# Picking the gathered tile's experts for four heads at once, with index lookups two slots innermost and a new pacing of the gate stage

## The chip, the cores and the metric

The kernel runs on one core of a Trainium2 chip. The metric is the device time of one execution in microseconds; the time given is the median of several runs. In all texts PE is TensorE, DVE is VectorE, ACT is ScalarE, POOL is GpSimd, SP is SyncE, the engine that issues most DMAs.

## What is computed

Two decoder layers over 512 tokens of width 1024 and 16 meta tokens ahead of them. A layer is a mixer (causal pooling in layer 0, stick-breaking attention in layer 1) and then a PEER expert network, which takes most of the time:

```python
def peer(h, w_query, sub_keys, u, v):          # 8 heads, 2 x 128 sub-keys, 16384 experts
    q = (h @ w_query).reshape(tokens, 8, 2, 128)
    s = einsum('thpc,hpnc->thpn', q, sub_keys)            # two rows of 128 scores a head
    top_s, top_i = lax.top_k(s, 16)
    cand_s = top_s[..., 0, :, None] + top_s[..., 1, None, :]          # 256 candidates
    cand_i = top_i[..., 0, :, None] * 128 + top_i[..., 1, None, :]
    best_s, best_pos = lax.top_k(cand_s, 16)
    expert = take_along_axis(cand_i, best_pos); gate = softmax(best_s)
    act = gelu(einsum('td,thkd->thk', h, u[expert]), approximate=False)
    return einsum('thk,thkd->td', gate * act, v[expert])
```

Each token so has 128 experts with a gate, 16 of each of 8 heads.

## The kernel before

**Two ways through the experts.** The 512 tokens are four tiles of 128. Tiles 0 to 2 are "dense": the products with all 16384 experts are formed on PE, and those not picked get a gate of zero. Tile 3 (`GATHERED`) and, in layer 0, the meta tokens fetch the rows of just the experts that were picked. A row, in the words of the program, is one slot of the gathered tile: 128 tokens' expert vectors u and v, 128x2048 f32, fetched by an indirect DMA that POOL issues (L343) into one of `NROW` = 4 buffers with at most three in flight; DVE forms the dot product `prod` with the tokens (L355), ACT its gelu `ga` (L359), DVE the weight `gwt` (L363) and the update `hx` of the residual (L367). The gathered tile has 128 rows a layer, the meta tokens 16. Four calls of `row_step` take one row through: fetch, dot, gelu, update.

**The query stage.** For each of 8 heads two projections (PE, `psu`, L510 and L511) are copied out by ACT (`qt`, L512, 3 buffers), and their product with the keys (`ps`, L524) is copied by ACT to `s` (L527, 3 buffers), of which DVE takes the top 16 of each of 8 rows of scores (`top16`, L393 to L397). After each head, tile 3's slots are picked (`select`, below), and some steps of rows are run. Between heads stand u steps (`u_step`, L314): 24 matmuls that form one block of 128 experts' products with the three dense tiles, of which the result goes to DRAM (`aout`). A weight of a projection or a u step is split into two parts, `w_hi` by ACT (L279) and `w_lo`, on POOL in the query stage (L283) and on DVE in the gate stage (L281), two buffers each. POOL's queue so holds the w_lo of the query stage and the gathers, in the order of the program.

**A pick.** `select` takes the sums of the two sorted lists that can be among the best 16 (80 of the 256, `cand`), their top 16 a head (values `bv`, positions `bp`), works out of the position the two ranks (`da`, `db`, some 14 small instructions), looks each rank up among the 16 indices of its list (a one-hot of 16 a slot, L442; its product with the indices, L445; a sum, L448), and forms the softmax gate. It is called once a head for tile 3 (16 slots), once for the meta tokens, and in the gate stage once for each dense tile (128 slots).

**The gate stage.** For each dense tile `build_gates` writes, 8 tokens at a time, two one-hots and a weighed one (`hot` L604, `weighed` L608 twice), from which PE forms the gates of all experts (`pg`, L588); they go through ACT (`stage`) to DRAM (`gout`). The stage is a generator that yields a planned cost after each piece: in a dense pick 3.0 twice, 3.5, 6.0 twice and 1.0 (22.5 in all), and 2.44 for each of the 16 groups of a tile (39 in all). The planner adds each cost times `DVE_SLACK` to `td`, and then issues quarters of u steps (`u_parts`, 24 matmuls in four parts) until their planned time `tu` reaches `td`; a u step is planned at `ucost` = 0.0111 x 384 = 4.26, and a gate group's PE work at 0.47 for four tokens. It runs row steps until `tr` reaches `td`; each adds `ROW_PERIOD[layer][0] / 8` to `tr` and 4.7 / 8 to `td`. Rows stop when fewer than `QUIET` = 8 groups are left. What DVE and PE do in this stage stands in each queue in the order that this sets.

**The v stage.** The u steps that are left (`late`) come each with two `v_step`s, the first three ahead; when no u step is left, v steps follow alone ("lone"). A v step loads 128 experts' v, their products and gates (`v32`, `ac2` and, for four blocks, `gt`, from SP's queue), splits them (`v_hi`, `v_lo`, `wt_hi`, `wt_lo`) and runs 18 matmuls (L705) into sums that stay in PSUM. Each step adds `ucost` to `tu`, and a row step `ROW_PERIOD[layer][1] / 8` to `tr`. After the last row the lone v steps go on without rows.

## Time and profile before

| what | value |
|---|---|
| median of 3 runs | 3092.58 us (3089.8 to 3094.88) |
| the profiled execution, device time | 3092.34 us |
| its span | 3090.6 us |
| mean granted clock of PE over the span | 0.979 |
| layer 0, query stage to the first gate product | 57 to 314 us |
| layer 0, gate stage | 314 to 656 us |
| layer 1, the same two | 1780 to 2038, 2038 to 2382 us |

The span runs from the first to the last instruction of the profiled execution, the device time a little beyond it on either side. Engines work side by side, so a busy share says which of them is near its limit over all, and not at which moment; for that the stretches are looked at one by one. The four stretches above are cut by the first gate product (`pg`) and the end of the gates' writing; what lies behind 656 us is layer 0's v stage and the attention, and behind 2382 us layer 1's v stage.

### The profile page before, as it was taken

How to read it: one execution, taken by the hardware profiler on the slowest of the kernel's cores; microseconds unless marked ns; L12 is line 12 of the kernel's file. 1: busy time of each engine (PE TensorE's matmuls, PEld its weight loads, DVE VectorE, ACT ScalarE, POOL GpSimd, SP SyncE). 2: the span in 40 equal slices, each digit the busy share in tenths (PEclk: the TensorE clock that was granted, in tenths of full speed). 3: DMA queues.
4: the chain of work that ended last, by engine and by line, in shares of the span. 5: the costliest groups of instructions: out<-in, count | busy, mean ns of one | idle time of the engine just before them, and what ended most of it. 6: DMA issues, size and time to landing. Idle time of an engine off the chain costs nothing.

```text
span 3090.6 us, 45463 instructions
## 1 busy us (share of the span) xinstructions
PE 2926.3 (95%) x16514; PEld 2609.5 (84%) x16514; DVE 2412.3 (78%) x5158; ACT 1344.7 (44%) x2190; POOL 694.7 (22%) x702
## 2 busy tenths in 40 slices
PE   8988899989999999999999989888999999999999
PEld 7887898988888888779965778788898888888887
DVE  3999999878878887856456469999987988888755
ACT  3443655643333333344455334454645433333333
POOL 3431221121212111004235244312211122121100
PEclk9999999999999999999999999999999999999999
DMA  3535789899999998942100344478878999999775
GB/s 128 181 122 205 288 286 336 295 347 351 338 324 335 334 348 291 316 148 82 56 1 1 109 156 146 166 279 277 319 291 315 391 326 337 324 341 342 256 226 170
DMA packets 290451, 763.61 MB, mean 247 GB/s; under 512 B 23601, under 2 KB 180529, under 8 KB 252081
## 3 DMA queue, kind: packets, MB, share of 16 engines
q1 hardware_dynamic: 224416, 393.48, 37.7%
q0 software_dynamic: 39168, 285.23, 25.0%
q10 hardware_dynamic: 26640, 82.00, 6.7%
q8 instruction: 129, 2.11, 0.3%
q14 instruction: 98, 0.79, 0.1%
HBM read 676.54 MB, written 84.08 MB: 246 GB/s over the span
## 4 chain that ended last, share of the span: by engine, by line
PE 71%; DVE 21%; issue 3%; DMA 2%; ACT 2%; POOL 0%; SPq 0%; DVEq 0%; ACTq 0%; POOLq 0%
PE y L705 32%; PE psu L314 24%; PE pp L124 2%; PE pp L125 2%; PE pp L123 2%; DVE w_lo L281 2%; PE pg L588 2%; DVE weighed L608 2%; DVE hot L604 2%; DVE prod L355 2%; DVE hx L367 1%; DVE mr L395 1%; DVE ti L397 1%; DVE ti L394 1%; DMA w<-in_peer_ut_dram 1%
## 5 line engine op out<-in xcount | busy, mean ns | idle before, releaser
L314 PE MATMUL psu<-n_hi,w_lo 128*128 128x384 f32 x2048 | 704.3, 344 | 66.5 <-DVE w_lo L281 66.5
L343 POOL DMA_INDIRECT row<-in_peer_uv_dram,ei x272 | 392.6, 1443 | 1641.8 <-DVE hx L367 1238.5
L314 PE MATMUL psu<-n_hi,w_hi 128*128 128x384 f32 x2048 | 713.2, 348 | 11.8 <-ACT ac L321 7.2
L314 PE MATMUL psu<-n_lo,w_hi 128*128 128x384 f32 x2048 | 704.8, 344 | 0.6 <-DVE n_lo L118 0.6
L279 ACT ACTIVATE w_hi<-w 128x1024 fp32r<-128x1024 f32 x288 | 304.9, 1060 | 471.1 <-PE psu L314 358.9
L705 PE MATMUL y<-v_hi,wt_hi 128*128 128x512 f32 x1536 | 474.9, 390 | 6.4 <-ACT wt_hi L697 5.8
L705 PE MATMUL y<-v_lo,wt_hi 128*128 128x512 f32 x1536 | 474.7, 390 | 2.2 <-DVE v_lo L691 2.0
L705 PE MATMUL y<-v_hi,wt_lo 128*128 128x512 f32 x1536 | 474.2, 390 | 0.0
L314 PEld LDWEIGHTS psu<-n_hi,w_lo 128*128 128x128 f32 x2048 | 395.2, 193 | 76.4 <-DVE w_lo L281 76.1
L314 PEld LDWEIGHTS psu<-n_hi,w_hi 128*128 128x128 f32 x2048 | 393.1, 192 | 17.7 <-ACT ac L321 8.0
L314 PEld LDWEIGHTS psu<-n_lo,w_hi 128*128 128x128 f32 x2048 | 394.0, 192 | 4.9 <-DVE n_lo L118 1.1
L697 ACT ACTIVATE wt_hi<-wt 128x384 fp32r<-128x384 f32 x256 | 134.4, 525 | 570.9 <-PE y L705 275.4
L698 DVE TENSOR_TENSOR wt_lo<-wt,wt_hi 128x384 fp32r<-128x384 f32 x256 | 142.5, 557 | 267.7 <-ACT wt_hi L697 267.5
L705 PEld LDWEIGHTS y<-v_lo,wt_hi 128*128 128x128 f32 x1536 | 288.5, 188 | 64.8 <-DVE v_lo L691 4.4
L705 PEld LDWEIGHTS y<-v_hi,wt_lo 128*128 128x128 f32 x1536 | 288.7, 188 | 60.9 <-DVE wt_lo L698 0.4
L705 PEld LDWEIGHTS y<-v_hi,wt_hi 128*128 128x128 f32 x1536 | 287.3, 188 | 60.5 <-ACT wt_hi L697 6.2
L367 DVE SCALAR_TENSOR_TENSOR hx<-row,gwt,hx 128x1024 f32<-128x1024 f32 x256 | 336.5, 1314 | 2.1
L355 DVE SCALAR_TENSOR_TENSOR prod<-row,hnat 128x1024 bf16<-128x1024 f32 x272 | 333.6, 1226 | 0.7 <-DMA row<-in_peer_uv_dram,ei 0.6
L281 DVE TENSOR_TENSOR w_lo<-w,w_hi 128x1024 fp32r<-128x1024 f32 x230 | 280.7, 1221 | 65.9 <-ACT w_hi L279 64.6
L691 DVE TENSOR_TENSOR v_lo<-v,v_hi 128x1024 fp32r<-128x1024 f32 x256 | 312.2, 1220 | 7.9 <-ACT v_hi L690 7.9
L690 ACT ACTIVATE v_hi<-v 128x1024 fp32r<-128x1024 f32 x256 | 270.5, 1056 | 23.5 <-DMA v<-in_peer_uv_dram 23.2
L593 ACT ACTIVATE stage<-pg 128x512 f32<-128x512 f32 x192 | 200.7, 1157 | 79.7 <-PE pg L588 77.3
(312 smaller groups left out, 4258.4 us busy)
## 6 DMA issues: line engine op xcount, KB each, us to landing
w<-in_peer_ut_dram SPq DMA_DIRECT2D x256, 512.0 KB
v<-in_peer_uv_dram SPq DMA_DIRECT2D x256, 512.0 KB
gout<-stage ACTq DMA_DIRECT2D x24, 2048.0 KB
gt<-gout SPq DMA_DIRECT2D x64, 768.0 KB
aout<-ac ACTq DMA_DIRECT2D x161, 192.0 KB
ac<-aout SPq DMA_DIRECT2D x161, 192.0 KB
w<-in_peer_wq_dram SPq DMA_DIRECT2D x32, 512.0 KB
wn<-in_w_kv_dram SPq DMA_DIRECT2D x8, 1024.0 KB
```

Of the source, the lines that this page charges most:

```text
L279: amark.append(sc.activation(whi, w, AF.Copy))
L281: vmark.append(v.tensor_sub(wlo, w, whi.bitcast(F32)))
L314: m = pin(pe.matmul(ps[:, :ND], a[:, k, :], b[:, k, c0:c0 + ND], start=st, stop=en))
L343: gp.indirect_dma_start(out=row, out_offset=None, in_=peer_uv, in_offset=bass.IndirectOffsetOnAxis(ap=item[1], axis=0))
L355: v.scalar_tensor_tensor(prod, row[:, :D], 1.0, hn_nat[i], ALU.mult, ALU.mult, accum_out=dot)
L367: v.scalar_tensor_tensor(acc, row[:, D:], wt, acc, ALU.mult, ALU.add)
L593: sc.activation(stage[:, :, o:o + 4].rearrange("p j t -> p t j"), pg, AF.Copy, scale=1.0 / GSCALE)
L690: amark.append(sc.activation(vhi, v32, AF.Copy))
L691: vmark.append(v.tensor_sub(vlo, v32, vhi.bitcast(F32)))
L697: sc.activation(whi, wt, AF.Copy)
L698: vmark.append(v.tensor_sub(wlo, wt, whi.bitcast(F32)))
L705: pe.matmul(y[n][half], wp[:, ts], vq[:, half * 512:(half + 1) * 512], start=st, stop=en)
```

## The change

**Picks.** Tile 3's slots are picked for four heads at once (`GH`), behind heads 3 and 7; the first row of tile 3 can so be fetched only when head 3 has its scores. The planner's allowance for rows is 26 for each of the heads from the fifth on, where it was 10.4 for every head.

**Lookups.** In all picks the ranks `da` and `db` become F16; the one-hot is laid out with two slots innermost, compared with `iota_x` (each number twice), and the indices `tib` are written twice as wide to fit; the product of 16 is halved by an addition before the reduction, whose input is half as long.

**Pacing.** The planned costs of a pick become 6.9, 5.6, 3.4, 4.6 twice and 1.2 (26.3 in all), `DVE_SLACK` 1.27; in the gate stage a row step adds 23 / 8 to `tr`, where it was 18 / 8, and 0.95 to `td`, where it was 4.7 / 8. The period of the v stage stays 13.5.

```diff
-DVE_SLACK = 1.35
+DVE_SLACK = 1.27
-ROW_PERIOD = ((18.0, 13.5), (18.0, 13.5))
+ROW_PERIOD = ((18.0, 23.0, 13.5), (18.0, 23.0, 13.5))
+GH = 4
...
             def gather_rows(i, h, i1, i2, gate, ns, acc, first):
-                ef = gr.tile([P, TK], F32, name="ef", bufs=2)
+                ef = gr.tile([P, GH * TK], F32, name="ef")[:, :ns]
                 v.tensor_scalar(ef, i1, float(NK), float(layer * NE), ALU.mult, ALU.add)
-                ei = gr.tile([P, TK], I32, name=f"ei{i}_{h}")
+                ei = gr.tile([P, ns], I32, name=f"ei{i}_{h}")
...
                         if h % 4 == 3:
-                            yield 3.0
-                    a, b, u, w = st("da"), st("db"), st("du"), st("dw")
+                            yield 6.9 if h == 3 else 5.6
+                    a, b, u, w = st("da", F16), st("db", F16), st("du"), st("dw")
...
-                    yield 3.5
-                    tib = tmp.tile([P, nh, 2, TK], F16, name=f"tib{nh}")
-                    v.tensor_copy(tib, tii)
+                    yield 3.4
+                    tib = tmp.tile([P, nh * 2, TK, 2], F16, name=f"tib{nh}")
+                    v.tensor_copy(tib, tii.rearrange("p h c a -> p (h c) a").unsqueeze(3).to_broadcast(
+                        [P, nh * 2, TK, 2]))
+                    t5 = tib.rearrange("p (h c) a b -> p h c (a b)", c=2)
...
-                        v.tensor_tensor(oh, iota_b.unsqueeze(1).to_broadcast([P, ns, TK]),
-                                        sel.unsqueeze(2).to_broadcast([P, ns, TK]), ALU.is_equal)
-                        o4 = oh.rearrange("p (h s) a -> p h s a", h=nh)
-                        v.tensor_tensor(o4, o4, tib[:, :, half, :].unsqueeze(2).to_broadcast([P, nh, TK, TK]),
-                                        ALU.mult)
+                        oh = flat.rearrange("p (n a b) -> p n a b", a=TK, b=2)
+                        v.tensor_tensor(oh, iota_x[:, :TK].unsqueeze(1).to_broadcast([P, ns // 2, TK, 2]),
+                                        sel.rearrange("p (n b) -> p n b", b=2).unsqueeze(2).to_broadcast(
+                                            [P, ns // 2, TK, 2]), ALU.is_equal)
+                        o4 = flat.rearrange("p (h n c) -> p h n c", h=nh, c=2 * TK)
+                        v.tensor_tensor(o4, o4, t5[:, :, half, :].unsqueeze(2).to_broadcast(
+                            [P, nh, TK // 2, 2 * TK]), ALU.mult)
+                        o3 = flat.rearrange("p (n c) -> p n c", c=2 * TK)
+                        v.tensor_add(o3[:, :, :TK], o3[:, :, :TK], o3[:, :, TK:])
                         ir = outp.tile([P, ns], F32, name=f"{tag}i{half}")
-                        v.tensor_reduce(ir, oh, AX.X, ALU.add)
+                        v.tensor_reduce(ir.rearrange("p (n b) -> p n b", b=2),
+                                        oh[:, :, :TK // 2, :].rearrange("p n a b -> p n b a"), AX.X, ALU.add)
                         res.append(ir)
-                        yield 6.0 * nh / H
+                        yield 4.6 * nh / H
...
-                    yield 1.0
+                    yield 1.2
...
-                        tq += 10.4
+                        tq += 26.0 if h >= GH else 0.0
...
-                        for i in gathered:
-                            res = []
-                            for _ in select(qp, gr, f"g{i}_{h}", tv[i][:, h:h + 1], ti[i][:, h:h + 1], 1, res):
-                                pass
-                            gather_rows(i, h, *res, TK, hx[i], False)
+                        if h % GH == GH - 1:
+                            hs = slice(h - GH + 1, h + 1)
+                            for i in gathered:
+                                res = []
+                                for _ in select(qp, gr, f"g{i}_{h}", tv[i][:, hs], ti[i][:, hs], GH, res):
+                                    pass
+                                gather_rows(i, h, *res, GH * TK, hx[i], False)
...
                     while tr < td and blocks[0] >= QUIET and row_step():
-                        tr += ROW_PERIOD[layer][0] / 8
-                        td += 4.7 / 8
+                        tr += ROW_PERIOD[layer][1] / 8
+                        td += 0.95
```

**What moves.** PE's instructions are the same in number (17,576 matmuls of the program); DVE's go from 4303 to 3952. By the order of the program the stages hold:

| | layer 0 before | now | layer 1 before | now |
|---|---|---|---|---|
| rows ahead of the first gate group / in the gate stage / in the v stage | 15 / 31 / 98 | 17 / 27 / 100 | 14 / 31 / 83 | 16 / 27 / 85 |
| u steps done ahead of the v stage, of 128 | 79 | 86 | 82 | 90 |
| w_lo on DVE ahead of the first group / in the gate stage / after | 13 / 59 / 46 | 15 / 64 / 39 | 10 / 59 / 43 | 12 / 65 / 35 |
| lone v steps with rows among them / rows there | 20 / 14 | 44 / 30 | 5 / 5 | 32 / 22 |
| v steps after the last row | 20 | 10 | 41 | 30 |

On POOL, in layer 0's query stage, the first rows of tile 3 (`ei_0`, head 0's slots) stand between the w_lo of early heads before:

```order
L283 TENSOR_TENSOR w_lo<-w_1183,w_hi 128x1024
L343 DMA row<-in_peer_uv_dram,ei_0_988 128x2048 x3
L283 TENSOR_TENSOR w_lo<-w_1217,w_hi 128x1024
L343 DMA row<-in_peer_uv_dram,ei_0_988 128x2048
L283 TENSOR_TENSOR w_lo<-w_1323,w_hi 128x1024
L343 DMA row<-in_peer_uv_dram,ei_0_988 128x2048
L283 TENSOR_TENSOR w_lo<-w_1383,w_hi 128x1024
```

Now the first rows (`ei_3`, the slots of heads 0 to 3) come behind the w_lo of head 5's first projection (`w_1872`), and that of its second (`w_1935`) behind five of them:

```order
L282 TENSOR_TENSOR w_lo<-w_1872,w_hi 128x1024
L342 DMA row<-in_peer_uv_dram,ei_3_1688 128x2048 x5
L282 TENSOR_TENSOR w_lo<-w_1935,w_hi 128x1024
L282 TENSOR_TENSOR w_lo<-w_1995,w_hi 128x1024
L342 DMA row<-in_peer_uv_dram,ei_3_1688 128x2048 x3
L282 TENSOR_TENSOR w_lo<-w_2147,w_hi 128x1024
```

Before, three gathers stood together at first and then one between two w_lo each; now five, then three, with buffers for four rows.

On DVE, in layer 0 before, one row is worked on inside each head's pick (here that of head 3: the lookup of `db`, then the row's update, then head 4's top 16):

```order
L355 SCALAR_TENSOR_TENSOR prod,dot<-row,hnat_88 128x1024
L442 TENSOR_TENSOR oh_1866<-iota_b,db 128x256
L445 TENSOR_TENSOR oh_1866<-oh_1866,tib_1859 128x256
L448 TENSOR_REDUCE g_3i_1869<-oh_1866 128x16
L334 TENSOR_TENSOR ei_3_1881<-ef,g_3i_1869 128x16
L363 TENSOR_TENSOR gwt<-ga,g_0gate 128x1
L367 SCALAR_TENSOR_TENSOR hx_76<-row,gwt,hx_76 128x1024
L393 MAX tv_633<-s 128x8 x2
```

Now the first rows come at the end of head 4's top 16, several in a row:

```order
L396 MAX_INDEX ti_638<-tv_634,mr_1860 128x8
L394 MATCH_REPLACE mr_1866<-tv_634,s 128x128
L354 SCALAR_TENSOR_TENSOR prod,dot<-row,hnat_87 128x1024
L395 MAX tv_634<-mr_1866 128x8
L354 SCALAR_TENSOR_TENSOR prod,dot<-row,hnat_87 128x1024
L396 MAX_INDEX ti_638<-tv_634,mr_1866 128x8
L362 TENSOR_TENSOR gwt<-ga,g_3gate 128x1 x2
L366 SCALAR_TENSOR_TENSOR hx_75<-row,gwt,hx_75 128x1024 x2
L354 SCALAR_TENSOR_TENSOR prod,dot<-row,hnat_87 128x1024
```

So the rows moved from the heads' picks to the end of a top 16 that is complete but for its last indices.

On DVE, late in layer 1's v stage, the lone v steps before have no row among them:

```order
L698 TENSOR_TENSOR wt_lo<-wt,wt_hi 128x384
L693 TENSOR_TENSOR wt<-ac_30021,gt 128x384
L691 TENSOR_TENSOR v_lo<-v_29957,v_hi 128x1024
L698 TENSOR_TENSOR wt_lo<-wt,wt_hi 128x384
L693 TENSOR_TENSOR wt<-ac_30053,gt 128x384
```

At the place that answers to it now the rows go on:

```order
L354 SCALAR_TENSOR_TENSOR prod,dot<-row,hnat_17483 128x1024
L699 TENSOR_TENSOR v_lo<-v_28702,v_hi 128x1024
L362 TENSOR_TENSOR gwt<-ga,g_7gate 128x1
L701 TENSOR_TENSOR wt<-ac_28779,gt 128x384
L366 SCALAR_TENSOR_TENSOR hx_75<-row,gwt,hx_75 128x1024
L706 TENSOR_TENSOR wt_lo<-wt,wt_hi 128x384
```

The u steps run out earlier, and the rows go on beside v steps alone.

## Rows read from the trace of the kernel before

**Rows 1.** The page's first part: busy time and instructions of each engine.

```profile
PE 2926.3 (95%) x16514; PEld 2609.5 (84%) x16514; DVE 2412.3 (78%) x5158; ACT 1344.7 (44%) x2190; POOL 694.7 (22%) x702
```

**Rows 2.** Stretches: length; busy PE, PEld, DVE, ACT, POOL; clock; DMA share; GB/s.

```profile
57.00:314.00 257.00, 222.41 (x1473) 217.44 (x1473) 230.04 (x1071) 102.65 (x180) 83.76 (x44) 0.93 0.48 166
314.00:656.00 342.00, 317.88 (x2252) 304.46 (x2250) 307.50 (x506) 196.25 (x263) 61.88 (x32) 0.98 0.84 304
1220.00:1283.00 63.00, 61.79 (x270) 50.21 (x269) 51.40 (x77) 22.92 (x38) 9.32 (x8) 1.00 0.93 322
1240.00:1280.00 40.00, 38.79 (x169) 31.16 (x168) 33.66 (x53) 15.67 (x26) 7.36 (x6) 1.00 0.98 341
...
2038.00:2382.00 344.00, 313.34 (x2212) 299.87 (x2211) 305.33 (x515) 195.72 (x261) 62.67 (x31) 0.97 0.83 296
2410.00:2450.00 40.00, 40.00 (x195) 35.30 (x194) 36.72 (x54) 15.81 (x26) 9.34 (x7) 1.00 1.04 398
```

**Rows 3.** PE's waits, 57 to 314: line, releaser: total us, times, longest.

```profile
PE ps L524 <- ACT qt L512: 15.7, 7, 5.1
PE psu L314 <- DVE w_lo L281: 14.0, 5, 7.8
PE psq L511 <- ACT w_hi L279: 4.3, 1, 4.3
```

**Rows 4.** PE's waits, 314 to 656.

```profile
PE psu L314 <- DVE w_lo L281: 17.6, 10, 3.1
```

**Rows 5.** DVE's waits, 314 to 656.

```profile
DVE w_lo L281 <- ACT w_hi L279: 24.3, 10, 7.0
```

**Rows 6.** DVE in time, head 2 of layer 0: start, us, line.

```profile
125.44 0.49 DVE L393 MAX8 tv<-s 128x8 f32<-128x128 f32 x2 [1.11 <-issue]
...
134.34 0.25 DVE L408 TENSOR_TENSOR cand<-tv 128x16 f32<-128x16 f32 x2
...
135.33 0.24 DVE L393 MAX8 bv<-cand 128x8 f32<-128x80 f32 x1
...
136.67 1.42 DVE L453 TENSOR_TENSOR dd<-bv 128x16 f32<-128x16 f32 x1
...
143.40 0.18 DVE L334 TENSOR_TENSOR ei<-ef,g_2i 128x16 int32<-128x16 f32 x1
...
143.68 3.28 DVE L367 SCALAR_TENSOR_TENSOR hx<-row,gwt,hx 128x1024 f32<-128x1024 f32 x1
```

**Rows 7.** DVE by shape, 57 to 403: count, busy us, mean ns.

```profile
L281 DVE TENSOR_TENSOR w_lo<-w,w_hi 128x1024 fp32r<-128x1024 f32 x26 | 31.6, 1220 | 2.8 <-ACT w_hi L279 2.6
L355 DVE SCALAR_TENSOR_TENSOR prod<-row,hnat 128x1024 bf16<-128x1024 f32 x23 | 28.0, 1218 | 0.6 <-DMA row<-in_peer_uv_dram,ei 0.6
L608 DVE TENSOR_TENSOR weighed<-hot,sl 128x1024 f16<-128x1024 f16 x32 | 20.6, 685 | 0.0
L604 DVE TENSOR_TENSOR hot<-iota_x,sl 128x2048 f16<-128x2048 f16 x16 | 19.4, 1220 | 0.0
L448 DVE TENSOR_REDUCE gdi<-hot 128x128 f32<-128x2048 f16 x3 | 6.8, 2279 | 0.0
...
L442 DVE TENSOR_TENSOR hot<-iota_b,da 128x2048 f16<-128x2048 f16 x2 | 4.6, 2284 | 0.0
```

**Rows 8.** In time: head 3's scores, an update, head 7's last index.

```profile
143.76 2.39 PE L524 MATMUL ps<-keys,qt 128*128 128x128 f32 x12 [1.89 <-ACT qt L512]
...
254.70 1.28 DVE L367 SCALAR_TENSOR_TENSOR hx<-row,gwt,hx 128x1024 f32<-128x1024 f32 x1
255.90 0.17 DVE L334 TENSOR_TENSOR ei<-ef,g_7i 128x16 int32<-128x16 f32 x1
```

**Rows 9.** POOL in time, beside the update of rows 6.

```profile
143.50 2.37 POOL L283 TENSOR_TENSOR w_lo<-w,w_hi 128x1024 fp32r<-128x1024 f32 x1 [5.44 <-ACT w_hi L279]
```

**Rows 10.** Chain of waits, layer 0's v stage: u step, two v steps.

```profile
668.60 4.23 PE psu L314 x24
672.83 8.18 PE y L705 x36
```

More of the change, by code (lines that the diff above doesn't have):

```diff
@@ L71, in trunk_kernel @@
     iota_x = const([P, P, 2], F16, "iota_x")
-    iota_b = const([P, TK], F16, "iota_b")
     own = const([P, AH], F32, "own")
@@ L139, in pool_mixer @@
             v.tensor_copy(iota_x, iota_f.unsqueeze(2).to_broadcast([P, P, 2]))
-            v.tensor_copy(iota_b, iota_f[:, :TK])
             for op, n, name in ((ALU.logical_shift_right, 4, "head"), (ALU.bitwise_and, NM - 1, "slot")):
@@ L437, in select @@
                     for half, sel in ((0, a), (1, b)):
                         if nh == H:
-                            oh = hot_tile().rearrange("p w a k b -> p (w a k b)").rearrange("p (n a) -> p n a", a=TK)
+                            flat = hot_tile().rearrange("p w a k b -> p (w a k b)")
                         else:
-                            oh = tmp.tile([P, ns, TK], F16, name=f"oh{nh}")
-                        v.tensor_tensor(oh, iota_b.unsqueeze(1).to_broadcast([P, ns, TK]),
-                                        sel.unsqueeze(2).to_broadcast([P, ns, TK]), ALU.is_equal)
@@ L444, in select @@
-                        o4 = oh.rearrange("p (h s) a -> p h s a", h=nh)
-                        v.tensor_tensor(o4, o4, tib[:, :, half, :].unsqueeze(2).to_broadcast([P, nh, TK, TK]),
-                                        ALU.mult)
+                            flat = tmp.tile([P, ns * TK], F16, name=f"oh{nh}")
+                        oh = flat.rearrange("p (n a b) -> p n a b", a=TK, b=2)
+                        v.tensor_tensor(oh, iota_x[:, :TK].unsqueeze(1).to_broadcast([P, ns // 2, TK, 2]),
+                                        sel.rearrange("p (n b) -> p n b", b=2).unsqueeze(2).to_broadcast(
+                                            [P, ns // 2, TK, 2]), ALU.is_equal)
@@ L728, in peer @@
                     while tr < tu and row_step():
-                        tr += ROW_PERIOD[layer][1] / 8
+                        tr += ROW_PERIOD[layer][2] / 8
                 while row_step():
```

## The prediction

> **What bounds the kernel now.** The page's first part comes first: TensorE (PE) is busy 2926.3 of 3090.6 us [rows 1]. The change adds and removes no matmul, so time can come only out of the 164 us in which PE is idle, or go into it. The table of stretches says where these are [rows 2]. PE lacks 34.6 us in 57 to 314 (layer 0, queries to the first gate product), 24.1 in 314 to 656 (its gate stage) and 30.7 in 2038 to 2382 (layer 1's gate stage); layer 1's query stage is built as layer 0's. In the v stage it lacks almost nothing.
>
> In the query stretch VectorE (DVE) is the bound: it is busy 230.0 of 257 us, and its idle time lies ahead of the first scores, while PE waits for copies (`qt` behind `s`) that DVE holds up, and then for w_lo behind DVE's picks [rows 3]. In the gate stretch neither engine is the bound all the time: PE waits 17.6 us for w_lo [rows 4], DVE 24.3 us for w_hi [rows 5], whose two buffers PE frees. They wait for each other in turn; what the planner charges for a piece decides who.
>
> **The price of a pick.** Head 2 of layer 0: from the first candidate row (134.34) to its indices (143.40) are 9.1 us, with one row's dot product of 1.2 inside, so 7.9 for a pick of one head; the top-16 of its scores take 8.9 (125.44 to 134.34) [rows 6]. A pick of four heads: top-16 of the candidates, 4 x 1.34 = 5.4 (135.33 to 136.67 in head 2); 25 small instructions of 64 columns at about 0.2, 5.0; two lookups. A lookup of 64 slots has 1024 columns: compare and multiply in F16 pairs are the form of weighed, 0.69 each; the halving sum has 512 columns, between 0.18 (a small instruction [rows 6]) and 0.69, taken as 0.43; the reduction of 512 lies between 0.18 and 2.28 (2048 columns), on the line through both at 0.70 [rows 7]. That is 2.5 a lookup. Sum 15.4, against 4 x 7.9 = 31.6. Eight single picks become two of four: DVE is relieved of 32 us a layer.
>
> A dense pick: the compare against an F32 slot number is 2.28, the same size with pairs innermost (hot from iota_x) 1.22; the multiply stays 1.22; the new sum of 1024 columns is 0.69, the reduction of 1024 by that line 1.22 instead of 2.28. A lookup falls from 5.8 to 4.35 [rows 7]; less 0.3 for the wider index copy, a pick is 2.6 shorter, three a layer. If the compare kept its F32 price, it would give back 2.1 a pick, 13 us of DVE over both layers.
>
> **Term A, queries to the first gate product.** 32 us less work do not come off. Heads 0 to 3 now have no pick: DVE needs 8.9 a head, PE about 18 (head 2's top-16 starts at 125.44 [rows 6], PE reaches head 3's scores at 143.76 [rows 8]), and DVE waits. PE gets there after 8.65 us of waits that DVE had caused (4.3 once and part of 15.7 [rows 3]); without them it is at 135, and the 2.4 of scores and the top-16 end at 146. From there DVE's chain is two picks (31), four top-16 (36), 11 rows at 2.5 (dot 1.22 [rows 7], update 1.28 [rows 8]; 28), two w_lo (2.4 [rows 7]), some 8 us of held instructions, and about 4 waiting for head 7: 255. Before, the same place in the order is at 255.9 [rows 8]. The held instructions: an update takes 3.28 us instead of 1.28 while POOL's w_lo (143.50, 2.37 us) runs [rows 6, 9]; I keep that at half of what eight heads show. The 4 us come from the order on POOL: head 5's second w_lo now stands behind five gathers, of which the fifth needs the first row's buffer back, and that row is worked on behind head 4's top-16. PE waits about 12 us there, and DVE, itself late, feels a third.
>
> From 256 to the first gate product takes 58 us before (the stretch ends with it, at 314); now 2.6 less for the pick, 2.5 more for a row, 2.4 more for two w_lo. So the first product comes 1 to 2 us later, but two more u steps (4.23 us each [rows 10]) are through by then: 8.5 less 2, say 6. Layer 1 has the same counts: 6. **A is 12.** Bounds: without held instructions and POOL's wait, 36; with twice of both, -12.
>
> **Term B, gate stages.** The planner's PE time against DVE's price for each piece, both with the u steps that the pace brings (4.26 planned a step, 1.2 of w_lo each):
> before, a pick 30.4 (22.5 x 1.35) against 27 (top-16 10.7, small ones 5, lookups 11.6) + 8.6 = 35.6; a tile's 16 gate groups 52.7 against 40 + 10.6 = 50.6; a row 2.35 against 2.5 + 0.7 = 3.2. With two picks, three tiles and 31 rows: PE 292, DVE 322.
> Now, a pick 33.4 (26.3 x 1.27) against 24.4 + 9.4 = 33.8; the groups 49.6 against 40 + 9.7 = 49.7; a row 3.8 against 2.5 + 1.1 = 3.6. With 27 rows: PE 318, DVE 314.
> Before, DVE was 30 us over, near the 24.1 and 30.7 that PE lacks; now the pieces match one by one. Some waiting for buffers stays: I take 8 in layer 0 and 13 in layer 1 (the end of its stage, where gate rows are written and read back, is not touched). **B is 16 + 17 = 33.** Bounds: 10, if the waits only change places, and 46, if nearly all go.
>
> **Term V, v stages.** 7 and 8 u steps that left are PE's and no loss by themselves. But a pair (one u, two v) spreads its DMA over 12.4 us and a lone v takes 4.1 [rows 10], while rows still come every 6 us. Lone v steps with rows beside them rise from 20 to 44 and from 5 to 32, with 30 and 22 rows among them. Such a step moves 0.92 MB (v, a, a quarter of four blocks' gates) and 0.68 of a row of 1.05 MB, by the shapes in the code: 1.63 MB, 399 GB/s at PE's pace. Of the lone v steps of before, 1240 to 1280, with rows, reached a DMA share of 0.98 and 341 GB/s, and PE lost 1.2 us in 40; a stretch of layer 1 with u steps reached 398 with no loss [rows 2]. The first ten or so ran on tiles loaded ahead. Price of each of the 34 + 22 beyond ten: below, nothing (398 GB/s); above, 0.69 (341 held); PE's loss in those ten is 0.12 a step, and with the lead used up it should be more: I take 0.3. 56 x 0.3 less the 1.2 that is there already is 15.6. **V is -16** (0 to -37).
> The Trainium skill's page "SBUF — State Buffer", section "A bandwidth-pool intuition that's wrong", gives about 358 GB/s between HBM and a core. By it, as an estimate, a lone v with rows would take 4.55 us, V would be -24 and the sum 3071. The trace does not agree with it as a ceiling: 398 over 40 us [rows 2].
>
> The start, the attention and the pair stretches keep their order. Sum: 3092.3 (the profiled execution, its span and 1.7 us around it; the median of the runs shown is 3092.6) - 12 - 33 + 16 = **3063**.
>
> **Rivals.**
> 1. Both stages balance better and DMA carries 398 GB/s: A 20, B 40, V 0: 3032. For it: DVE's waits vanish with PE's when the pace fits. Against: POOL's blocked w_lo.
> 2. The pacing does not fit: the waits for w_lo only turn into other waits for w_lo, B 10: 3085; with B half-way, 3075. For it: rows bunch on DVE however the planner spaces them. Against: every piece above matches within 0.4.
> 3. DMA holds at 341 GB/s in lone v steps with rows: V -37, 3084. The mean of 1220 to 1283 was 322 at a share of 0.93 [rows 2], but PE lost only 1.2 us there. The page's limit above lies on this side too.
> 4. Slower: the same place, decided at 331 GB/s. A and B together are 45; a price of 0.83 on 56 steps eats them (4.92 us for 1.63 MB). At 322 GB/s it is 0.97: V -53, 3100. For it: the row 322. Against: that stretch was not short of data all the time.
> 5. The lookups do not become cheaper: 13 us of DVE, of which PE sees perhaps half: 3070, inside the forecast's range.
>
> **How the numbers follow.** About 0.2% (6 us) is what a measurement of this kernel can tell from no change. Forecast, 3044 to 3080: 0.60. Rival 1: 0.13. Rival 2: 0.12, all but 0.02 of it faster. Rival 3: 0.08, a third of it within 0.2%. Rival 4: 0.07, with 0.01 near zero. Faster 0.88, same 0.06, slower 0.06. The range that leaves out the ends of rivals 1 and 4 is 3032 to 3090.
>
> **What would show it.** In the new profile: DVE with gaps before the top-16 of heads 1 to 3 and nearly none after; one PE wait of some 12 us for POOL's w_lo in head 5 of each layer; the first gate product at 314 to 318 in layer 0; lookup compares of 1.22 (2048) and 0.69 (1024); PE idle in the two gate stages near 8 and 13; v stages some 30 us shorter for the u steps that left, with PE waits for v tiles of about 17 us in all between the last u step and the last row. The forecast is wrong if the gate stages keep more than 15 us of PE idle each, if the first product comes more than 10 us later, or if lone v steps with rows take over 4.6 us.

## The result and the profile after

The changed kernel takes 3076.04 us (median of 5 runs, 3071.0 to 3080.23) against 3092.58 before: ratio 0.9944, 95% interval 0.9927 to 0.9961. A later measurement gave 3078.27 (12 runs, e8 below), ratio 0.9962 (0.9951 to 0.9972). So it is faster by 12 to 17 us, some 0.5%, where 29 were forecast. The profiled execution, 3071.0 us, is the fastest of its five, so the stages below account for 21.3 us of span, some 5 more than the medians show.

The page of the changed kernel answers to [rows 1]: PE's busy time falls by 12 us with the same matmuls, DVE's by 91.

```profile
PE 2914.3 (95%) x16514; PEld 2597.2 (85%) x16514; DVE 2321.5 (76%) x4807; ACT 1313.3 (43%) x2154; POOL 664.3 (22%) x702
```

The table of stretches of the changed kernel, cut at the first u step of a layer, the first gate product, the first and the last v matmul (columns as in [rows 2]):

```profile
55.80:314.30 258.50, 223.02 (x1521) 218.99 (x1521) 205.57 (x950) 89.87 (x167) 89.90 (x46) 0.93 0.51 179
314.30:672.00 357.70, 335.42 (x2354) 323.13 (x2354) 291.15 (x448) 203.12 (x269) 44.40 (x27) 0.97 0.80 286
672.00:1366.80 694.80, 687.77 (x3218) 593.12 (x3217) 566.32 (x826) 263.69 (x436) 114.74 (x101) 1.00 0.92 329
...
1767.00:2031.50 264.50, 233.61 (x1189) 210.02 (x1189) 195.56 (x891) 88.06 (x136) 99.30 (x51) 0.95 0.51 179
2031.50:2392.80 361.30, 337.01 (x2366) 324.57 (x2365) 293.24 (x445) 203.22 (x269) 48.39 (x28) 0.98 0.79 284
2392.80:3064.10 671.30, 669.95 (x3120) 577.24 (x3120) 525.94 (x761) 253.11 (x408) 101.32 (x81) 1.00 0.89 317
```

The stretches of the kernel before, with the same cuts (layer 0's query stage, 256.8 us from 57.2, is the first of [rows 2]):

```profile
314.00:652.10 338.10, 313.99 (x2235) 301.29 (x2234) 305.53 (x504) 196.25 (x263) 61.88 (x32) 0.98 0.84 303
652.10:1378.10 726.00, 717.51 (x3386) 623.91 (x3385) 568.80 (x823) 272.73 (x447) 121.84 (x98) 1.00 0.89 316
1779.90:2038.20 258.30, 226.83 (x1141) 203.99 (x1141) 224.54 (x997) 101.82 (x148) 97.81 (x49) 0.95 0.48 169
2038.20:2384.70 346.50, 315.84 (x2223) 302.51 (x2222) 307.83 (x517) 195.72 (x261) 63.68 (x32) 0.97 0.83 296
2384.70:3086.20 701.50, 701.35 (x3313) 609.69 (x3311) 529.53 (x759) 263.39 (x421) 99.14 (x79) 1.00 0.86 303
```

Lengths can't be compared as they are, since u steps moved between stages (2 more in each query stage, 5 and 6 more in the gate stages, 7 and 8 fewer in the v stages, at 4.23 us [rows 10]). With them taken out, the gain is: query stages 6.8 and 2.3 us, gate stages 1.6 and 10.6, v stages 1.6 and -3.6; the start, the stretch between the layers and the end make up the other 2. These are single executions, and a stage of the same kernel differs by up to 7 us from one to the next: cut the same way, e8's execution of the changed kernel (span 3074.6 us) gives 5.7 and 2.0, -5.2 and 14.4, 7.8 and -7.5. The sums over both layers (9, 12 and -2; in e8 8, 9 and 0) can be relied on more than the layers' shares.

### The profile page after: what moved, and what is told of

The parts are those of the page before. It is cut to its first block, busy times and chain, and to the rows that moved or that the text cites. A ratio compares the mean times of both kernels' runs of the same rounds, so it can differ in the third digit from the quotient of the medians.

```text
span 3069.3 us, 45150 instructions
## 1 busy us (share of the span) xinstructions
PE 2914.3 (95%) x16514; PEld 2597.2 (85%) x16514; DVE 2321.5 (76%) x4807; ACT 1313.3 (43%) x2154; POOL 664.3 (22%) x702
## 4 chain that ended last, share of the span: by engine, by line
PE 76%; DVE 15%; DMA 5%; ACT 2%; issue 2%; POOL 1%; SPq 0%; DVEq 0%; ACTq 0%; POOLq 0%
PE y L713 30%; PE psu L313 27%; DMA v<-in_peer_uv_dram 3%; PE pp L124 2%; PE pp L125 2%; PE pp L123 2%; PE pg L596 2%; DVE w_lo L280 2%; DVE prod L354 1%; PE psq L517 1%; PE psu L516 1%; DVE hx L366 1%; DVE weighed L616 1%; DVE hot L612 1%; DVE mr L394 1%
## 5 line engine op out<-in xcount | busy, mean ns | idle before, releaser
L342 POOL DMA_INDIRECT row<-in_peer_uv_dram,ei x272 | 363.8, 1337 | 1767.5 <-DVE hx L366 1492.2
L366 DVE SCALAR_TENSOR_TENSOR hx<-row,gwt,hx 128x1024 f32<-128x1024 f32 x256 | 329.6, 1287 | 2.6
```

What stands on the lines that cost most here:

```text
L342: gp.indirect_dma_start(out=row, out_offset=None, in_=peer_uv, in_offset=bass.IndirectOffsetOnAxis(ap=item[1], axis=0))
L366: v.scalar_tensor_tensor(acc, row[:, D:], wt, acc, ALU.mult, ALU.add)
```

## The experiments

Each kernel is compared with the kernel before on the same chip.

**The three parts of the change, each with and without the others.** e1 is the changed kernel with the old planner numbers, e2 with the old lookups, e3 with a pick after every head; e4, e9 and e10 are the kernel before with one part alone.

```diff
-DVE_SLACK = 1.27
+DVE_SLACK = 1.35
-ROW_PERIOD = ((18.0, 23.0, 13.5), (18.0, 23.0, 13.5))
+ROW_PERIOD = ((18.0, 18.0, 13.5), (18.0, 18.0, 13.5))
-                        td += 0.95
+                        td += 4.7 / 8
```

```diff
-GH = 4
+GH = 1
-                        tq += 26.0 if h >= GH else 0.0
+                        tq += 10.4
```

(The first diff is e1's, the second e3's, both cut. e1 also has the old costs in `select`; e3 also gives `ef` its two buffers back; e2 has the lines of `select` that the diff of the change shows as removed, and the `iota_b` that they read; the other three combine these edits.)

> The changed kernel with the planner's old numbers (costs of a pick 3.0, 3.0, 3.5, 6.0, 6.0, 1.0; DVE_SLACK 1.35; row period 18 and 4.7/8 a row step in the gate stage). 79 and 82 u steps ahead of the v stage again, as before the change. My theory: the query stages keep the 9 us that the picks of four gave, the gate stages lose the 12 that they gained, the v stages get back 2: about 3085 us, with PE idle 20 to 27 us in each gate stage. Rival (the pace decides nothing, the work taken off DVE everything): 3076, as the changed kernel. Second rival (the pace is all of the gain): 3092.

> The changed kernel with the index lookups as they were (F32 ranks, one-hot of 16 with a slot's numbers innermost, a reduction of full size), in picks of four too. DVE gets 1.4 x 2 x 3 = 8.7 us a layer more in the dense picks and some 4 in the picks of four. My theory: DVE is late where these stand (end of the query stage, first third of the gate stage), so PE sees about half: 3086 us. Rival (the dense picks lie in DVE's waits, which grew to 43 us for w_hi in the gate stage): 3078 or less.

> The changed kernel with a pick after every head again (GH 1, allowance 10.4 for rows after every head), new lookups and new pacing kept. 16 us of DVE a pick of four become 4 x 7.3, so some 26 us more a layer in the query stage. My theory: the first gate product comes 10 to 14 us later in each layer than in the changed kernel, less 4 where PE's waits for copies let u steps fit: 3076 + 2 x 8 = 3092. Rival (the query stage gave nothing, since its end is set by PE's single wait of 19 us for w_lo that the picks of four caused): 3076 or faster.

> The kernel before with the new lookups alone (picks after every head, old pacing). DVE is relieved of 8.7 us in the dense picks and about 3 in the single picks a layer. My theory: as DVE is late in both stages, PE sees half: 3092 - 11 = 3081 to 3086. Rival (pieces are charged as before, so only waits grow): 3090 to 3093.

> The kernel before with picks of four heads alone (old lookups, old pacing; the allowance for rows of the query stage goes with the picks). With the new lookups the picks of four were worth 9 us under the old pacing (3088 to 3079) and 11 to 13 under the new. My theory: they act on the query stage and do not depend on the rest: 3091 - 9 = 3082 us. Rival (they need the short lookups, since DVE's work at the end of the query stage sets the wait for its first w_lo): 3091.

> The kernel before with the new pacing alone (picks after every head, old lookups). By the sums of the prediction a pick would be charged 33.4 us of PE against 36.4 of DVE, less short than before the change (30.4 against 35.6), so the kernel would be no slower than before: 3091. My theory now: what counts is the piece at the end of a pick; a lookup charged 4.6 x 1.27 = 5.8 takes 5.8 and 1.6 of w_lo, two of them in a row, and PE waits for their results at the transposes and then runs slow for some us: the new pacing costs about 25 us without the new lookups, as it did with picks of four: 3110 us, with 10 us or more of PE waiting for gdi in the gate stages.

| lookups | picks | pacing | run | median us | ratio, 95% |
|---|---|---|---|---|---|
| new | single | old | e4 | 3088.06 | 0.9990 (0.9979 to 1.0000) |
| old | of four | old | e9 | 3099.30 | 1.0022 (1.0012 to 1.0033) |
| old | single | new | e10 | 3101.06 | 1.0039 (1.0026 to 1.0051) |
| new | of four | old | e1 | 3079.03 | 0.9965 (0.9952 to 0.9979) |
| new | single | new | e3 | 3089.36 | 0.9988 (0.9976 to 1.0001) |
| old | of four | new | e2 | 3105.22 | 1.0050 (1.0030 to 1.0069) |
| new | of four | new | changed kernel (e8) | 3078.27 | 0.9962 (0.9951 to 0.9972) |

The parts do not add up. By the medians, alone the lookups are worth 3 us, the picks of four cost 8, the pacing costs 10 (the kernel before beside them: 3090.9 to 3091.1); picks and lookups together gain 12, and the pacing adds 1 to 6 to that (by the ratios of e8 and of the first measurement); since the intervals of e1 and e8 overlap, it is not shown that the pacing gains anything in the whole change. Of my expectations e3 came near (3 us); e1 was 6 too high and lies nearer to its rival, that the pace decides nothing (3076); e4 lies 2 above its range and 2 below its rival's; e2 was 19 us too low, e9 failed outright (a loss, not a gain of 9), and e10 was 9 too high. The rival of e9, that the picks need the short lookups, stands.

Why the picks need them is seen where the second pick of four ends in layer 0's query stage, first in e1, then in e9, which differ in the lookups alone (DVE's last index of head 7, and the wait of PE behind it):

```profile
244.59 0.22 DVE L333 TENSOR_TENSOR ei<-ef,g_7i 128x64 int32<-128x64 f32 x1
250.12 0.69 PE L313 MATMUL psu<-n_hi,w_lo 128*128 128x384 f32 x1 [19.26 <-DVE w_lo L280]
```

```profile
248.77 0.21 DVE L335 TENSOR_TENSOR ei<-ef,g_7i 128x64 int32<-128x64 f32 x1
254.31 0.69 PE L315 MATMUL psu<-n_hi,w_lo 128*128 128x384 f32 x1 [20.05 <-DVE w_lo L282]
```

With the old lookups both come 4.2 us later, and the first gate product comes 7.1 us later (316.6 against 309.5): the work of DVE at the end of the query stage sets the wait for its first w_lo, as the rival said. The place on POOL's queue that the prediction named is not the reason. There e9 waits once, 13.2 us for the w_lo, and e1 twice, 6.7 us for a copy of `qt` and 5.0 for the w_lo; both go on at nearly the same time (176.5 and 175.6).

Why the pacing gains less without them is seen in PE's waits for a dense pick's result (`gdi`, for the transposes of `build_gates`), of e2, e10 and the changed kernel over the whole span:

```profile
PE ps L566 <- DVE gdi L449: 13.3, 4, 5.1
```

```profile
PE ps L566 <- DVE gdi L449: 12.1, 6, 2.9
```

```profile
PE ps L571 <- DVE gdi L453: 3.4, 2, 2.7
```

A lookup that takes DVE 5.8 us is charged at 4.6, which the factor 1.27 makes 5.8 us of PE's work, with nothing for the w_lo that DVE forms in the meantime; so it is late at the end of the pick, where PE waits for it, whatever the sum over the pick says. And a wait costs more than its length. e2's gate stages, with the same matmuls as the changed kernel's, are 10.7 and 8.6 us longer, but PE idles only 5.6 and 1.3 us more in them; the rest is busy time at a lower granted clock (0.95 and 0.96 instead of 0.97 and 0.98):

```profile
317.70:686.10 368.40, 340.56 (x2354) 327.55 (x2354) 303.03 (x470) 203.10 (x268) 42.03 (x28) 0.95 0.77 279
2048.90:2418.80 369.90, 344.31 (x2366) 332.40 (x2366) 302.31 (x468) 203.31 (x269) 46.29 (x28) 0.96 0.77 275
```

In e10 the loss lies elsewhere. With the moved u steps taken out, its query stages are 6 us shorter than those of the kernel before, its gate stages 1, and its v stages, with 7 and 8 u steps fewer, 7.0 and 16.1 us longer:

```profile
683.50:1386.90 703.40, 692.35 (x3217) 595.73 (x3218) 569.51 (x835) 265.21 (x438) 121.86 (x103) 0.99 0.91 329
2414.70:3098.50 683.80, 672.74 (x3121) 578.00 (x3120) 529.10 (x769) 253.01 (x409) 104.88 (x84) 0.99 0.88 316
```

e3, which has the new lookups, loses as much in the v stages (2.2 and 20.9) but gains 15 in the gate stages. So the old lookups took from the pacing what it gains in the gate stages, and its price lies in the v stages with either lookups. Why the changed kernel does not pay that price is open.

**e5, the wait at the end of the query stage.** In the changed kernel PE stops once for 19 us before the first gate product, for the first w_lo that DVE forms (PE's timeline):

```profile
250.53 0.69 PE L313 MATMUL psu<-n_hi,w_lo 128*128 128x384 f32 x1 [19.25 <-DVE w_lo L280]
```

e5 puts four u steps ahead of it:

```diff
+                    for _ in range(4 if layer == 0 else 4):
+                        plan.append(("u", nu))
+                        nu += 1
                     plan.append(("u", nu))
                     plan.reverse()
```

> The changed kernel with four more u steps at the end of the query stage's plan in both layers (behind head 7's projections, so with w_lo on POOL): 90 and 94 u steps ahead of the v stage. My theory: PE's single wait of 19.3 us in layer 0 (231 to 250, for the first w_lo that DVE forms, which stands behind head 7's top 16 and the second pick of four) and the 17 us of such waits in layer 1 are idle time that four u steps of 4.23 us fill; the first gate product comes at the same time with four more u steps done, and the slow stretch of PE's clock behind the wait goes too. Gain 17 in layer 0, 12 in layer 1, less 1 for more lone v steps with rows: 3048 us. Rival: POOL's four more w_lo hold DVE's instructions (2 us each, as the update of 3.28 us showed before), the first product comes 8 us later in each layer: 3062. Second rival: the wait only moves behind the four u steps, with nothing gained: 3076.

Measured: 3073.17, ratio 0.9944 (0.9927 to 0.9961), beside 3078.27 for the changed kernel (e8). The single wait fell from 19.25 to 7.20 us. The first product came at 322.0, 7.7 us later than 314.3, with four more u steps done (16.9), so 9 us were gained in layer 0, and layer 1's query stage took 4.9 more for the same 16.9, a gain of 12. The rival's delay of 8 us was there, but the sum of 21 was not in the time: the v stages gave most back. In the profile layer 1's v stage was 6 us shorter with four u steps less, where 16.9 were due. The rows of e5 for the lone v steps with rows of layer 0 and of layer 1:

```profile
1106.40:1336.00 229.60, 222.68 (x969) 180.44 (x969) 194.68 (x292) 86.56 (x140) 37.08 (x31) 1.00 0.97 351
2775.70:2953.50 177.80, 173.57 (x751) 139.55 (x751) 150.20 (x227) 66.62 (x109) 25.32 (x24) 1.00 1.00 356
```

The DMA share is at 0.97 to 1.00, and PE loses 6.9 and 4.2 us there, 4 more than in the changed kernel. Another 6.1 us are lost among layer 1's pairs, in a wait for `wt_hi` (the changed kernel has 4.5 us of it just ahead of the stage).

**e11, the same with layer 1's rows spread over its v stage.**

```diff
-ROW_PERIOD = ((18.0, 23.0, 13.5), (18.0, 23.0, 13.5))
+ROW_PERIOD = ((18.0, 23.0, 13.5), (18.0, 23.0, 15.0))
```

> The changed kernel with four more u steps at the end of the query stage and the rows of layer 1's v stage spread further (period 15.0 instead of 13.5, so that 11 instead of 26 v steps are left behind the last row). My theory: the query stages keep the 9 and 12 us that the four u steps gave, and of the 10 us that PE lost in layer 1's v stage, where DMA stood at a share of 0.93 to 1.00, some 5 come back: 3068 us. Rival (the waits there do not come from the rate of the rows): 3073.

Measured: 3058.26, ratio 0.9896 (0.9880 to 0.9911). Layer 1 took 4.2 us less than in e5 (1292.3 against 1296.5 from its first u step to its last v matmul), near what I expected, but a difference that two executions of one kernel show as well. The rest of the difference to e5 is not explained by the edit: in the two profiled executions 7.8 us lie between the layers, where the programs are the same (below).

**e6 and e7, two numbers of the pacing.** e6 sets `DVE_SLACK` to 1.34; e7 sets the v stage's period to 12.0.

> The changed kernel with DVE_SLACK 1.34 instead of 1.27: 91 and 94 u steps ahead of the v stage, so 5 and 4 more in the gate stages. My theory: the remaining 22 and 24 us of PE's idle time there are local, since DVE's instructions of a pick stand in bunches ahead of single w_lo while the average matches; more u steps a piece then buy nothing, idle 20 to 26 each, 3074 to 3080 us. Rival (PE is given too little work a piece): idle falls by some 8 us in each gate stage, 3060.

> The changed kernel with rows 12% closer in the v stages (period 12.0 instead of 13.5, a row every 5.4 us instead of 6). A pair with its rows then moves 4.6 MB in 12.4 us, 371 GB/s, and fewer lone v steps have rows. My theory: the DMA carries up to some 400 GB/s, the pairs lose nothing or little, the 5.8 and 1.3 us that PE idles in lone v steps with rows shrink: 3070 to 3076 us. Rival (a limit near 358 GB/s): each of some 75 pairs takes 0.45 us more, 3076 + 34 - 5 = 3105; a limit at the 341 GB/s that the pairs show now would give still more.

> The changed kernel itself, as a yardstick on the same chip beside the three others: 3076 us, ratio to the kernel before 0.993 to 0.996.

Measured: e6 3080.58, ratio 0.9964 (0.9949 to 0.9979); e7 3082.44, 0.9976 (0.9965 to 0.9986); e8 3078.27. In e6, PE's idle time in the gate stages fell from 22.3 and 24.3 to 18.8 and 18.7 us, below my range though not as far as the rival's, and nothing was gained in time: with the moved u steps taken out, this execution's gate stages are 5 and 7 us shorter than the changed kernel's, and its v stages 1 and 7 longer. In e7 the pairs became slower, against my expectation (480.2 and 434.4 us where the changed kernel has 472.3 and 424.6, and e8 470.9 and 427.9), by half of what the rival said; the execution is the slowest of twelve (3091.4), and the median is only 4 us above e8's, with intervals that overlap:

```profile
673.60:1153.80 480.20, 475.14 (x2282) 417.66 (x2282) 406.63 (x598) 180.02 (x311) 115.91 (x82) 1.00 0.96 356
2397.90:2832.30 434.40, 426.00 (x2041) 375.56 (x2042) 364.74 (x538) 162.19 (x279) 101.63 (x74) 0.99 0.96 354
```

Asked for 371 GB/s, the DMA gave 354 to 356 over more than 400 us.

**e12, room for DVE to work ahead in the gate stage.** In the changed kernel the waits of PE and then of DVE in layer 0's gate stage answer to [rows 4] and [rows 5]:

```profile
PE psu L313 <- DVE w_lo L280: 16.0, 8, 5.5
```

```profile
DVE w_lo L280 <- ACT w_hi L278: 43.1, 24, 7.5
DVE hot L612 <- PE pg L596: 13.8, 9, 2.3
```

DVE now has 57 us to spare, and still PE waits 16.0 us for w_lo. The longest, 5.48 us, ends at 387.5. ACT had the `w_hi` that this w_lo needs ready at 378.9, and DVE formed the w_lo 7.3 us later. The timeline ahead of it, ACT's `w_hi` first: on DVE small instructions of the next tile's pick and gate work, one after the other without a gap, and the w_lo behind them:

```profile
377.85 1.05 ACT L278 ACTIVATE w_hi<-w 128x1024 fp32r<-128x1024 f32 x1
...
380.34 0.22 DVE L395 MAX8 bv<-mr 128x8 f32<-128x80 f32 x1
...
382.75 1.26 DVE L616 TENSOR_TENSOR weighed<-hot,sl 128x1024 f16<-128x1024 f16 x2
...
386.22 1.22 DVE L280 TENSOR_TENSOR w_lo<-w,w_hi 128x1024 fp32r<-128x1024 f32 x1
```

And PE's, behind it: the matmuls of a u step, which begin every 0.176 us as a rule (24 in 4.23), begin every 0.32 us for the next 3 us, at a granted clock of 0.50 (1.2 GHz, half of the full 2.4):

```profile
387.49 0.69 PE L313 MATMUL psu<-n_hi,w_lo 128*128 128x384 f32 x1 [5.48 <-DVE w_lo L280]
387.97 0.52 PE L313 MATMUL psu<-n_hi,w_hi 128*128 128x384 f32 x1
388.29 0.52 PE L313 MATMUL psu<-n_lo,w_hi 128*128 128x384 f32 x1
```

```profile
387.50:390.80 3.30, 3.30 (x10) 3.05 (x10) 2.47 (x4) 0.00 (x0) 1.68 (x1) 0.50 0.53 175
```

```diff
-NROW = 4
+NROW = 3
...
-                whi = up.tile([P, KC, P], F32R, name="w_hi", bufs=2)
-                wlo = up.tile([P, KC, P], F32R, name="w_lo", bufs=2)
+                whi = up.tile([P, KC, P], F32R, name="w_hi", bufs=3)
+                wlo = up.tile([P, KC, P], F32R, name="w_lo", bufs=3)
...
-                for kk in (key, following):
+                more = ()
+                if gating[0] and following is not None and following[1] + 1 < NK:
+                    more = (("u", following[1] + 1),)
+                for kk in (key, following, *more):
```

> The changed kernel with three buffers of w_hi and w_lo instead of two and, in the gate stage, a weight asked for two u steps ahead instead of one; for the room, rows have three buffers instead of four (two in flight). My theory of the 22 and 24 us that PE still idles in the gate stages: DVE's instructions of the next pick stand in bunches ahead of single w_lo, and with two buffers DVE cannot work ahead; with three the 16 us of waits for w_lo in each gate stage fall below 8, and the stages get 8 to 10 us shorter each for the same work: 3058 to 3065 us, if two rows in flight cost nothing. Rival (DVE has too much work in these stages, wherever it stands): the waits for w_lo stay at 12 to 16 us a stage, 3076 to 3080.

Measured: 3040.17 us, ratio 0.9836 (0.9817 to 0.9856), 18 us better than the low end of what I expected; the profiled execution took 3049.53. The gate stages of e12, with the same u steps as the changed kernel's, are 15.2 and 22.4 us shorter:

```profile
307.80:650.30 342.50, 329.32 (x2353) 320.09 (x2352) 296.20 (x496) 202.93 (x269) 57.98 (x27) 0.99 0.82 297
2019.30:2358.20 338.90, 330.75 (x2366) 321.23 (x2364) 296.57 (x506) 202.86 (x271) 44.19 (x27) 0.99 0.83 300
```

No wait for w_lo is left in layer 0's gate stage; in layer 1's, where the changed kernel has 15.6 us of them, one is left:

```profile
PE psu L316 <- DVE w_lo L280: 0.2, 1, 0.2
```

The granted clock there is 0.99 instead of 0.97 and 0.98: of the 15.2 and 22.4 us, 9.1 and 16.1 are idle time and 6.1 and 6.3 are PE's own pace. The query stages are 7.6 and 10.4 us shorter as well (the third buffer is there too), and the v stages 17.7 and 13.3 longer (712.5 and 684.6 us), which I put down to the rows' lost buffer without a run that shows it alone. The third buffer, the earlier request and the fewer rows in flight were not run apart, so which of them took the waits away is not shown; nor was e12 run with e5's or e11's edit.

## Why the prediction was right in sign and range, and half wrong inside

The time lay in the range and the sign was right, but that the time lay there was in part luck, since the two largest errors went against each other: the gate stages gained 12 us where 33 were put down, and the v stages lost 2 where 16 were.

**The prices of a pick held.** DVE by shape in the changed kernel, answering to [rows 7]: compare 1.22 and 0.68 (forecast 1.22 and 0.69), product of 1024 columns 0.68 (0.69), halving sum of 512 0.42 (0.43), reduction of 1024 columns 1.21 (1.22), of 512 0.68 (0.70).

```profile
L453 DVE TENSOR_REDUCE gdi<-hot 128x128 f32<-128x1024 f16 x12 | 14.6, 1214 | 0.1
...
L444 DVE TENSOR_TENSOR hot<-iota_x,da 128x2048 f16<-128x2048 f16 x6 | 7.3, 1220 | 0.2 <-PE pg L596 0.2
...
L448 DVE TENSOR_TENSOR oh<-oh,tib 128x1024 f16<-128x1024 f16 x8 | 5.4, 680 | 0.0
L451 DVE TENSOR_TENSOR oh<-oh 128x512 f16<-128x512 f16 x8 | 3.3, 418 | 0.1
L444 DVE TENSOR_TENSOR oh<-iota_x,da 128x1024 f16<-128x1024 f16 x4 | 2.7, 684 | 0.0
```

**Term A, 12 forecast, 9 measured.** The order of events was right. DVE waits in the first heads (42.3 us for scores between 80 and 314, where it waited 13.0 before), the 32 us do not come off, and the first gate product comes at 314.3, in the forecast 314 to 318, with two more u steps through. Before and now:

```profile
DVE tv L393 <- ACT s L527: 13.0, 2, 12.6
```

```profile
DVE tv L392 <- ACT s L533: 42.3, 5, 12.6
```

PE's waits in the same stage (answering to [rows 3]), and DVE's timeline where the second pick of four is done (to [rows 8]):

```profile
PE psu L313 <- DVE w_lo L280: 20.5, 3, 19.3
PE ps L530 <- ACT qt L518: 7.4, 2, 6.6
PE psu L516 <- POOL w_lo L282: 5.0, 1, 5.0
```

```profile
244.99 0.22 DVE L333 TENSOR_TENSOR ei<-ef,g_7i 128x64 int32<-128x64 f32 x1
```

Inside it two steps erred against each other: head 7's last index is there at 245.0, not 255, and from there to the first product are 69 us, not 58 to 60: DVE forms 15 w_lo there instead of 11, and top 16 of the next tiles' picks take 9 us more. Of the 12 us for POOL's w_lo, 5.0 were that and 6.6 a wait for a copy of `qt` just ahead. What I did not see at all is the single wait of 19.25 us at the end of the stage: PE, no longer held up by copies, reached the end of its plan early and stood there. The waits that the picks of four took away came back as that one; e5 shows that it can be filled. So the idle time that the term priced did not fall in layer 0 (34.4 us of 256.8 before, 35.5 of 258.5 now). What was gained there is pace: PE is busy 222.4 us before and 223.0 now with the matmuls of two more u steps in it, and it stops 9 times where it stopped 15 times, which I read as fewer slow stretches behind the stops; no run shows that alone.

**Term B, 33 forecast, 12 measured: the step that failed.** "Now the pieces match one by one" was true of DVE's time for each piece and wrong as a reason for no waits. DVE's instructions do not stand piece by piece; those of the next pick stand between gate groups, ahead of a w_lo that PE needs now, and with two buffers of w_lo DVE can make up for it neither before nor after. So both engines wait, 16 and 57 us, though neither has too much to do. e1, with the planner's old numbers, has 8 of the 12 us in its gate stages already; e6 (another average) gained nothing in time; e12 took the waits for w_lo away, but it changed three things at once, so that a third buffer was what DVE lacked is likely and not shown. The prediction's own test, that more than 15 us of idle in each gate stage would prove it wrong, was met: 22.3 and 24.3.

**Left out of the sum: the clock.** Rows of the kernel before showed a granted clock of 0.93 to 0.98 in the stages with waits and 1.00 elsewhere [rows 2], and I priced only idle time. Behind waits of 3.45, 5.48 and 19.25 us in the changed kernel, PE ran at a granted clock of 0.50 for some 3 us, so a wait saved is worth more (e12: 37.6 us shorter gate stages for 25.2 us less idle), and a wait added costs more (e2).

**Rival 5 was mispriced.** It let PE see half of what DVE loses. e2 gives DVE some 12 us a layer back, so by that rule 12 us in all; it takes 27 more than the changed kernel (3105.2 against 3078.3, each beside the kernel before at 3091). In the gate stages, where 19 us of the two profiles' difference lie, the lookups stand where PE waits for their result, and the clock comes on top.

**Term V, -16 forecast, -2 measured: a price too high for this kernel.** PE idles 5.8 and 1.3 us in the 44 and 32 lone v steps with rows, 0.09 a step, not 0.3 beyond the tenth:

```profile
1144.30:1325.00 180.70, 174.95 (x755) 141.45 (x755) 150.60 (x228) 66.83 (x109) 24.18 (x24) 0.99 0.98 346
2817.40:2940.20 122.80, 121.50 (x535) 99.64 (x534) 105.73 (x161) 47.92 (x77) 15.95 (x16) 1.00 0.98 354
```

By their length, against 4.09 us for each 18 v matmuls, they took some 10 us more, 0.14 a step. That only 2 were lost in all is luck too: layer 0 got back a wait of 5.8 us at the start of its v stage. In e3 and e10, with the same pacing, the v stages lost 23 us, so the price was not too high for every kernel. The bytes per step were right, but not what the stretch had to move. The issues of the stretch 1144 to 1325 in the changed kernel (line, count, KB, us to landing) are 40 v, 38 a, 10 groups of gates and 24 rows for 44 v steps and 30 rows in the order:

```profile
v<-in_peer_uv_dram SPq DMA_DIRECT2D x40, 512.0 KB, 8.0
gt<-gout SPq DMA_DIRECT2D x10, 768.0 KB, 9.3
ac<-aout SPq DMA_DIRECT2D x38, 192.0 KB, 7.8
row<-in_peer_uv_dram,ei POOLq DMA_INDIRECT x24, 8.9
```

The others had been loaded ahead, so 346 GB/s did where I asked for 399. Whether 398 GB/s [rows 2] could have been held is a question of length. Whole stretches of pairs or of lone v steps with rows, 100 us and more at a DMA share of 0.96 to 1.00, show 332 (e3) to 362 GB/s (e12), but parts of them hold more, as 180 us of e6 do:

```profile
1130.00:1310.00 180.00, 177.01 (x766) 141.98 (x765) 156.26 (x233) 69.12 (x112) 30.45 (x27) 1.00 1.02 375
```

The Trainium skill's page "SBUF — State Buffer", section "A bandwidth-pool intuition that's wrong (but worth ruling out)", gives about 358 GB/s between HBM and a core. The 480 us of e7 at 356 GB/s are near it, and the 180 us above lie 5% over it, so as a ceiling over such a length the runs do not bear it out, and the prediction's sentence against it stands. In the changed kernel the full DMA cost PE little; e5, with more such steps, lost 4 us more in them.

**Open.** The time between the layers differs in profiles of kernels that are the same there: 395 us in e3 and e11, 397 in e4, 400 to 403 in the others. In e5 PE waits once for 5.3 us for `n_lo` at its start, in e11 the longest such wait is 1.6. What decides it was not found; it may be part of the spread of single runs (3074.6 to 3091.0 for e8).

## What to carry to other kernels

When two engines feed each other through two buffers, equal averages for each piece of the plan do not keep them from waiting: look in the trace at what stands directly ahead of the instruction that is waited for, and try a third buffer for the pair, with its request a step earlier, before the planner's numbers are tuned again. Price a wait of the matmul engine by the length of the stage and not by its idle time, since the engine ran at half clock for some us behind each of the waits looked at. And measure the parts of a combined change in combination, stage by stage: here picks of four and the pacing were each a loss without the shorter lookups, the one in the query stages, the other in the v stages.

## What the runs showed of the hardware

- **PE's clock.** After 5.48 us without a matmul, matmuls of 384 columns began every 0.32 us instead of every 0.176 for 3 us, at a granted clock of 0.50 (1.2 GHz).
- **DMA.** 40 us ran at 398 GB/s and 180 us at 375; the whole stretches of 100 us and more at a share of 0.96 to 1.00 ran at 332 to 362, and 480 us at 356.
